# Sharing the re-layout of two inputs among three engines in a batched X times Y-transposed kernel

## The chip, the cores and the metric

The kernel runs on one core of one Trainium2 chip. The metric is the time of one execution on the device in microseconds (us); of several executions the median is given. Engines are called as in the profile: PE is TensorE, DVE is VectorE, ACT is ScalarE, POOL is GpSimd, SP is SyncE, which here only issues transfers (DMA).

## The reference

```python
batch, n_heads, seq_t, seq_s, channels = 8, 12, 512, 512, 64
def reference(x, y):
    return np.einsum('bhtc,bhsc->bhts', x, y).astype(np.float32)
```

For each of 96 heads a 512 x 64 matrix is multiplied with the transpose of another. The inputs are 12.6 MB each, the output 100.7 MB, all float32.

## The kernel before

**Groups and slots.** The 96 heads go in 12 groups of 8. The x and the y of a group are loaded by two transfers of 1 MB into one slot of 16 KB per partition (`load`, L63), x in the first half and y in the second. A head lies on 16 partitions, so a group fills 128. There are five slots (`SLOTS`, L37). Results are collected in slots of the same pool: a result is 2 MB, one slot, one store.

**From a slot to the matmul.** `compress(g)` (L69) casts x to bf16 on ACT (L73, `xk`) and y to bf16 on DVE (L74, `yk`), both 128 partitions x 2048. After that the slot may be used again. Each group has two half groups of four heads (partitions 0 to 63 and 64 to 127); half group i is half i % 2 of group i // 2. `mix(i)` (L77) copies, on GpSimd, the channels of a half group into a layout in which two 32-channel halves lie on different partitions. For x these are four copies of 32 partitions x 1024 (L87) into `xb`, one of two tiles that were zeroed at the start and are used again by every second half group. For y these are two copies of 64 partitions x 1024 (L94) into `yb`. In `xb` and `yb` two bf16 values share one 32-bit word, and `transposes(i)` (L100) then transposes 32 x 32 blocks of words on DVE (L103 for x, L108 for y) into `xT` and `yT`. It also starts the mixing of half group i + 2.

**Results.** A half group gives two results, o = 2i and 2i + 1 (`result(o)`, L115). A result takes eight matmuls, in pairs into four PSUM tiles. ACT copies three of these tiles into a slot (L130) and DVE one (L128). An even result is followed by `transposes(i + 2)` on DVE. Then SP stores the slot (L133).

**Order.** All engines run their instructions in the order in which the program writes them. The five first loads come first (L136). Then for each group (L141): `compress`, at group 0 the mixing of half groups 0 and 1, at groups 2 and 4 the transposes of half groups 0 and 1, a further load at groups 0 to 4, 6 and 8, and results 0, 1 and 2 at groups 5, 7 and 9. The stores of these three results are issued only after the last load (L154). From there the results go one after the other, each with its store (L156). All loads and stores are on SP's queue.

Of the kernel before, what the change touches and what calls it, by code (L numbers as in the profile page):

```python
# [1 line left out]

# [4 lines left out]


@with_exitstack
def kernel(  # L10
    ctx: ExitStack,
    tc: tile.TileContext,
    x: bass.AP,
    y: bass.AP,
    out: bass.AP,
):

    nc = tc.nc
    B, H, T, C = x.shape
    _, _, S, _ = y.shape
    P = 128
    G = 8  # L30
    Q = P // G
    R = T // Q
    NG = B * H // G
    K = 8
    E = R // K
    D = 32
    SLOTS = 5  # L37
    fp32 = mybir.dt.float32
    bf16 = mybir.dt.bfloat16
    u32 = mybir.dt.uint32  # L40
    COPY = mybir.ActivationFunctionType.Copy
    assert C == 2 * D and S == T and R == D and Q * 2 == D

    xv = x.rearrange("b h t c -> (b h t c)").rearrange("(g p n) -> g p n", p=P, n=R * C)
    yv = y.rearrange("b h t c -> (b h t c)").rearrange("(g p n) -> g p n", p=P, n=R * C)
    ov = out.rearrange("b h t s -> (b h t s)").rearrange(
        "(o u h q n) -> o h q u n", u=2, h=2, q=Q * E, n=K * S
    )

    const = ctx.enter_context(tc.tile_pool(name="const", bufs=1))  # L50
    kept = ctx.enter_context(tc.tile_pool(name="kept", bufs=NG))
    slots = ctx.enter_context(tc.tile_pool(name="slots", bufs=SLOTS))
    ybpool = ctx.enter_context(tc.tile_pool(name="ybpool", bufs=2))
    tpool = ctx.enter_context(tc.tile_pool(name="tpool", bufs=3))
    pmpool = ctx.enter_context(tc.tile_pool(name="pmpsum", bufs=4, space=bass.MemoryType.PSUM))

    loaded, inputs, mixed, made = {}, {}, {}, {}
    zeroed = [const.tile([P, K * E * D], u32, name=f"xb{half}") for half in range(2)]

    def slot():  # L60
        return slots.tile([P, K * S], fp32, name="slot")

    def load(g):  # L63
        both = slot()
        nc.sync.dma_start(both[:, :R * C], xv[g])  # L65
        nc.sync.dma_start(both[:, R * C:], yv[g])  # L66
        loaded[g] = both

    def compress(g):  # L69
        both = loaded.pop(g)  # L70
        xk = kept.tile([P, R, C], bf16)
        yk = kept.tile([P, R, C], bf16)
        nc.scalar.activation(xk.rearrange("p r c -> p (r c)"), both[:, :R * C], COPY)  # L73
        nc.vector.tensor_copy(yk.rearrange("p r c -> p (r c)"), both[:, R * C:])  # L74
        inputs[g] = (xk, yk)

    def mix(i):  # L77

        g, half = divmod(i, 2)
        xk, yk = inputs[g]  # L80
        xb = zeroed[half]
        xv2 = xb.bitcast(bf16).rearrange("p (k e c u) -> p k e c u", k=K, e=E, u=2)
        base = half * 64
        for ch in range(2):
            for u in range(2):
                lo = base + u * D
                nc.gpsimd.tensor_copy(  # L87
                    xv2[(2 * ch + u) * D:(2 * ch + u + 1) * D, :, :, :, u],
                    xk[lo:lo + D, :, ch * D:(ch + 1) * D].rearrange("p (e k) c -> p k e c", k=K),
                )  # L90
        yb = ybpool.tile([P, R // 2 * D], u32)
        yv2 = yb.bitcast(bf16).rearrange("p (j c w) -> p j w c", j=R // 2, w=2)
        for ch in range(2):
            nc.gpsimd.tensor_copy(  # L94
                yv2[ch * 64:(ch + 1) * 64],
                yk[base:base + 64, :, ch * D:(ch + 1) * D].rearrange("p (j w) c -> p j w c", w=2),
            )
        mixed[i] = (xb, yb)

    def transposes(i):  # L100
        xb, yb = mixed.pop(i)
        xT = tpool.tile([P, K * D * E], u32)
        nc.vector.transpose(  # L103
            xT.rearrange("p (k r e) -> p k e r", k=K, e=E),
            xb.rearrange("p (k e c) -> p k e c", k=K, e=E),
        )
        yT = tpool.tile([P, D * R // 2], u32)
        nc.vector.transpose(  # L108
            yT.rearrange("p (r j) -> p j r", r=D), yb.rearrange("p (j c) -> p j c", c=D)
        )  # L110
        made[i] = (xT.bitcast(bf16).rearrange("p (k h m) -> p k h m", k=K, h=2), yT.bitcast(bf16))
        if i + 2 < 2 * NG:
            mix(i + 2)

    def result(o):  # L115

        i, h = divmod(o, 2)
        xT, yT = made[i]
        otf = slot()
        ot = otf.rearrange("p (r s) -> p r s", s=S)  # L120
        for k in range(0, K, 2):
            pm = pmpool.tile([P, 2, S], fp32)
            for two in range(2):
                nc.tensor.matmul(  # L124
                    pm[:, two, :], xT[:, k + two, h, :], yT[:, h * S:(h + 1) * S], start=True, stop=True
                )
            if k == 4:
                nc.vector.tensor_copy(ot[:, k:k + 2, :], pm)  # L128
            else:
                nc.scalar.activation(ot[:, k:k + 2, :], pm, COPY)  # L130
        if h == 0 and 2 <= i + 2 < 2 * NG:
            transposes(i + 2)
        return lambda: nc.sync.dma_start(ov[i, h], otf)  # L133

    with tc.manual_schedule():
        for g in range(SLOTS):  # L136
            load(g)
        nc.vector.memset(zeroed[0], 0.0)  # L138
        nc.gpsimd.memset(zeroed[1], 0.0)  # L139
        stores = []  # L140
        for g in range(NG):  # L141
            compress(g)
            if g == 0:
                mix(0)
                mix(1)
            if g in (2, 4):
                transposes(g // 2 - 1)
            if g < 5:
                load(g + SLOTS)
            elif g in (5, 7, 9):  # L150
                stores.append(result(len(stores)))
            elif g in (6, 8):
                load(g // 2 + 7)
        for store in stores:  # L154
            store()
        for o in range(len(stores), 4 * NG):  # L156
            result(o)()


# [1 line left out]
_INS = ['x', 'y']  # L161
_OUTS = [((8, 12, 512, 512), 'float32')]


# [23 lines left out]
```

## Time and profile before

| what | value |
|---|---|
| median of 5 runs | 303.24 us (302.9 to 303.28) |
| the profiled execution | 303.24 us, its span 301.0 us |
| bytes read and written | 25.17 MB and 100.66 MB, 418 GB/s over the span |
| L73 ACT cast of x, x12 | 1.91 us each |
| L74 DVE cast of y, x12 | 1.20 to 2.07 us each |
| L87 POOL copy of x, x96 | 135.5 us, 1.41 us mean |
| L94 POOL copy of y, x48 | 66.0 us, 1.38 us mean |
| L103 and L108 DVE transposes, x24 each | 2.07 and 1.06 us each |
| L130 ACT eviction, x144 | 1.02 us each |
| L128 DVE eviction, x48 | 1.22 us each |
| store, from issue to landing | 21.7 us at the median |

The span runs from the first to the last instruction of the profiled execution; the rest of its time lies around it. Busy time is that of the instructions of an engine; a group of instructions is one line of the program with one shape. The share of the transfer engines is the mean over the core's 16.

### The profile page before, as it was taken

The numbers are of one execution on the slowest core, as the hardware profiler recorded it, in microseconds if no ns is written. First come the engines' busy times: TensorE is split into PE (matmuls) and PEld (weight loads), VectorE is DVE, ScalarE is ACT, GpSimd is POOL, SyncE is SP. The second block draws the span as 40 slices with busy tenths as digits, with TensorE's granted clock in tenths as the row PEclk, the third lists the DMA queues.
The fourth block names the chain that finished last, engine by engine and source line by source line (L and its number), as shares of the span: only waits on it lengthen the run. The fifth ranks groups of instructions, "written<-read, shape, count | busy, mean of one in ns | idle before, by whom it ended". The sixth has DMA issues, their size and how long they took to land.

```text
span 301.0 us, 1574 instructions
## 1 busy us (share of the span) xinstructions
PE 138.2 (46%) x384; PEld 47.0 (16%) x384; DVE 147.1 (49%) x109; ACT 160.8 (53%) x157; POOL 202.6 (67%) x149
## 2 busy tenths in 40 slices
PE   0004124467465556454647554646564658652000
PEld 0001001112121212121212121212121212210000
DVE  1465962857375546653574357535653475313000
ACT  4252567697473747465655465655556564647000
POOL 1999999998997887779776977797779720000000
PEclk9999999569758697786897689778779765779555
DMA  7999999999999999999999999999999999999993
GB/s 290 427 422 422 422 422 422 420 442 425 437 427 425 440 418 438 433 427 438 422 431 439 422 431 431 427 444 418 433 434 425 435 431 420 434 427 425 427 438 144
DMA packets 10377, 125.93 MB, mean 418 GB/s; under 512 B 1152, under 2 KB 1152, under 8 KB 1152
## 3 DMA queue, kind: packets, MB, share of 16 engines
q1 hardware_dynamic: 10368, 125.83, 98.5%
q8 instruction: 3, 0.05, 0.1%
q14 instruction: 6, 0.05, 0.0%
HBM read 25.17 MB, written 100.66 MB: 418 GB/s over the span
## 4 chain that ended last, share of the span: by engine, by line
DMA 82%; ACT 7%; issue 3%; DVE 0%; ACTq 0%; SPq 0%
DMA out_dram<-slot 65%; DMA slot<-in_y_dram 17%; ACT slot L130 7%; DVE yk L74 0%; ACTq L183 0%; SPq L65 0%; SPq L66 0%; ACTq L130 0%
## 5 line engine op out<-in xcount | busy, mean ns | idle before, releaser
L124 PE MATMUL pm<-yT,xT 128*128 128x512 bf16 x384 | 138.2, 513 | 136.3 <-ACT slot L130 112.6
L130 ACT ACTIVATE slot<-pm 128x1024 f32<-128x1024 f32 x144 | 137.0, 1024 | 95.1 <-DMA out_dram<-slot 86.2
L87 POOL COPY xb<-xk 32x1024 bf16<-32x1024 bf16 x96 | 135.5, 1411 | 37.0 <-DVE xT L103 27.4
L128 DVE COPY slot<-pm 128x1024 f32<-128x1024 f32 x48 | 58.8, 1224 | 101.5 <-DMA out_dram<-slot 98.8
L124 PEld LDWEIGHTS <-xT 128*128 128x128 bf16 x384 | 47.0, 122 | 227.1 <-issue 191.8
L94 POOL COPY yb<-yk 64x1024 bf16<-64x1024 bf16 x48 | 66.0, 1375 | 2.9
L103 DVE STREAM_TRANSPOSE xT<-xb 128x1024 uint32<-128x1024 uint32 x24 | 49.6, 2066 | 0.0
L73 ACT ACTIVATE xk<-slot 128x2048 bf16<-128x2048 f32 x12 | 23.0, 1913 | 22.2 <-DMA slot<-in_x_dram 22.2
L74 DVE CAST yk<-slot 128x2048 bf16<-128x2048 f32 x12 | 19.7, 1639 | 27.6 <-DMA slot<-in_y_dram 27.6
L108 DVE STREAM_TRANSPOSE yT<-yb 128x512 uint32<-128x512 uint32 x24 | 25.4, 1058 | 0.0
L73 ACT ACT_TABLE_LOAD x1 | 1.3, 1283 | 0.7 <-PEq L172 0.7
L138 DVE MEMSET xb<- 128x1024 uint32 x1 | 0.9, 912 | 1.0 <-PEq L172 1.0
L139 POOL MEMSET xb<- 128x1024 uint32 x1 | 1.0, 952 | 0.3 <-POOLq L172 0.3
L172 POOL MEMSET const-float32-0.0<- 128x1 f32 x1 | 0.1, 98 | 0.2 <-issue 0.2
L172 POOL MEMSET const-float32-1.0<- 128x1 f32 x1 | 0.1, 98 | 0.0
L172 POOL MEMSET const-bfloat16-1.0<- 128x1 bf16 x1 | 0.1, 98 | 0.0
L172 POOL MEMSET const-uint8-127<- 128x1 uint8 x1 | 0.1, 98 | 0.0
## 6 DMA issues: line engine op xcount, KB each, us to landing
out_dram<-slot SPq DMA_DIRECT2D x48, 2048.0 KB, 21.7
slot<-in_x_dram SPq DMA_DIRECT2D x12, 1024.0 KB, 18.2
slot<-in_y_dram SPq DMA_DIRECT2D x12, 1024.0 KB, 19.2
```

Of the source, the lines that this page charges most:

```text
L73: nc.scalar.activation(xk.rearrange("p r c -> p (r c)"), both[:, :R * C], COPY)
L74: nc.vector.tensor_copy(yk.rearrange("p r c -> p (r c)"), both[:, R * C:])
L87: nc.gpsimd.tensor_copy(xv2[(2 * ch + u) * D:(2 * ch + u + 1) * D, :, :, :, u], xk[lo:lo + D, :, ch * D:(ch + 1) * D].rearrange("p (e k) c ...
L94: nc.gpsimd.tensor_copy(yv2[ch * 64:(ch + 1) * 64], yk[base:base + 64, :, ch * D:(ch + 1) * D].rearrange("p (j w) c -> p j w c", w=2),)
L103: nc.vector.transpose(xT.rearrange("p (k r e) -> p k e r", k=K, e=E), xb.rearrange("p (k e c) -> p k e c", k=K, e=E),)
L108: nc.vector.transpose(yT.rearrange("p (r j) -> p j r", r=D), yb.rearrange("p (j c) -> p j c", c=D))
L124: nc.tensor.matmul(pm[:, two, :], xT[:, k + two, h, :], yT[:, h * S:(h + 1) * S], start=True, stop=True)
L128: nc.vector.tensor_copy(ot[:, k:k + 2, :], pm)
L130: nc.scalar.activation(ot[:, k:k + 2, :], pm, COPY)
L138: nc.vector.memset(zeroed[0], 0.0)
L139: nc.gpsimd.memset(zeroed[1], 0.0)
L172: nc = _bacc.Bacc("TRN2", target_bir_lowering=False, num_devices=1)
```

## The change

- `compress(g)` no longer casts y into `yk`. It casts y from the slot straight into `yb`, the layout that `mix` made before, for both half groups, in four pieces of 64 partitions x 1024: two on DVE, one on GpSimd, one on ACT (`in_front`). `yb` is kept for all groups, in the place of `yk`, and `ybpool` goes.
- `mix` copies x alone, and is told which engines to use and which channel halves to do.
- Half groups 0 to 5 are mixed by GpSimd alone, in the loop over the groups: half group g // 2, channel half g % 2, so two copies per group, behind GpSimd's cast of y.
- Half groups 6 to 23 are mixed after an odd result, half group i + 4 after the second result of half group i: two copies on DVE, one on GpSimd, one on ACT (`behind`).
- `transposes(i)` starts no mixing any more. The transposes of half groups 2 and up stay after even results.

```diff
-    ybpool = ctx.enter_context(tc.tile_pool(name="ybpool", bufs=2))
...
+    in_front = [nc.vector, nc.gpsimd, nc.vector, nc.scalar]
+    behind = [nc.vector, nc.gpsimd, nc.scalar, nc.vector]
+    FIRST = NG // 2
+
+    def copy(engine, dst, src):
+        if engine is nc.scalar:
+            nc.scalar.activation(dst, src, COPY)
+        else:
+            engine.tensor_copy(dst, src)
...
     def compress(g):
         both = loaded.pop(g)
         xk = kept.tile([P, R, C], bf16)
-        yk = kept.tile([P, R, C], bf16)
         nc.scalar.activation(xk.rearrange("p r c -> p (r c)"), both[:, :R * C], COPY)
-        nc.vector.tensor_copy(yk.rearrange("p r c -> p (r c)"), both[:, R * C:])
-        inputs[g] = (xk, yk)
+        inputs[g] = xk
+        ys = both[:, R * C:].rearrange("p (r c) -> p r c", c=C)
+        for half in range(2):
+            yb = kept.tile([P, R // 2 * D], u32, name=f"yb{half}")
+            yv2 = yb.bitcast(bf16).rearrange("p (j c w) -> p j w c", j=R // 2, w=2)
+            for ch in range(2):
+                copy(
+                    in_front[2 * half + ch],
+                    yv2[ch * 64:(ch + 1) * 64],
+                    ys[half * 64:(half + 1) * 64, :, ch * D:(ch + 1) * D].rearrange(
+                        "p (j w) c -> p j w c", w=2
+                    ),
+                )
+            mixed[2 * g + half] = yb
 
-    def mix(i):
+    def mix(i, engines, halves=(0, 1)):
...
-        for ch in range(2):
+        for ch in halves:
             for u in range(2):
-                lo = base + u * D
-                nc.gpsimd.tensor_copy(
+                lo = half * 64 + u * D
+                copy(
+                    engines[2 * ch + u],
                     xv2[(2 * ch + u) * D:(2 * ch + u + 1) * D, :, :, :, u],
                     xk[lo:lo + D, :, ch * D:(ch + 1) * D].rearrange("p (e k) c -> p k e c", k=K),
                 )
-        yb = ybpool.tile([P, R // 2 * D], u32)
-        yv2 = yb.bitcast(bf16).rearrange("p (j c w) -> p j w c", j=R // 2, w=2)
-        for ch in range(2):
-            nc.gpsimd.tensor_copy(
-                yv2[ch * 64:(ch + 1) * 64],
-                yk[base:base + 64, :, ch * D:(ch + 1) * D].rearrange("p (j w) c -> p j w c", w=2),
-            )
...
     def transposes(i):
-        xb, yb = mixed.pop(i)
+        xb, yb = zeroed[i % 2], mixed.pop(i)
...
-        if i + 2 < 2 * NG:
-            mix(i + 2)
...
-        if h == 0 and 2 <= i + 2 < 2 * NG:
+        if h == 0 and i + 2 < 2 * NG:
             transposes(i + 2)
+        elif h == 1 and FIRST <= i + 4 < 2 * NG:
+            mix(i + 4, behind)
...
             compress(g)
-            if g == 0:
-                mix(0)
-                mix(1)
+            mix(g // 2, [nc.gpsimd] * 4, (g % 2,))
```

## The prediction

> **What bounds the kernel now.** I read the page's first two parts, then the stage table, then the queue of transfers, then the load stage in order of time. The page first: busy time by engine, the row of transfer engines in 40 slices, and the share of the one queue that moves data.
>
> ```profile
> PE 138.2 (46%) x384; PEld 47.0 (16%) x384; DVE 147.1 (49%) x109; ACT 160.8 (53%) x157; POOL 202.6 (67%) x149
> ...
> DMA  7999999999999999999999999999999999999993
> ...
> q1 hardware_dynamic: 10368, 125.83, 98.5%
> ```
>
> No compute engine is over 67% busy, while the transfer engines are over 90% busy in 38 of 40 slices. The stage table (busy us and count per engine, then clock, DMA share, GB/s):
>
> ```profile
> 0.00:4.00 4.00, 0.00 (x0) 0.00 (x0) 0.91 (x1) 1.28 (x1) 1.15 (x5) 1.00 0.52 168
> 4.00:24.00 20.00, 1.27 (x4) 0.55 (x5) 9.50 (x6) 7.64 (x4) 15.96 (x11) 1.00 1.02 426
> 24.00:60.00 36.00, 12.94 (x30) 4.20 (x29) 23.11 (x17) 21.59 (x16) 34.92 (x21) 0.91 1.01 422
> ...
> 80.00:244.00 164.00, 92.45 (x267) 31.62 (x266) 87.48 (x66) 94.47 (x100) 132.22 (x101) 0.78 1.01 431
> 244.00:292.00 48.00, 19.63 (x52) 6.43 (x50) 12.87 (x11) 20.27 (x22) 0.00 (x0) 0.64 1.00 427
> 292.00:301.00 9.00, 0.00 (x0) 0.00 (x0) 0.00 (x0) 0.00 (x0) 0.00 (x0) 0.50 0.46 197
> ```
>
> Between 4 and 292 us the transfer engines are full. In the stage 244 to 292 GpSimd does nothing at all and the rate is 427 GB/s, against 431 before it: relieving GpSimd does not speed the transfers. All bytes stay the same, so only a hole in the stream of transfers can change the time by much. I therefore look for the place where the stream is nearest to a hole. That is the end of the load stage, in SP's queue, where each line is start, length, issuing line:
>
> ```profile
> 32.89 0.33 SPq L66 DMA_DIRECT2D slot<-in_y_dram  x1
> 40.35 0.33 SPq L65 DMA_DIRECT2D slot<-in_x_dram  x1
> 40.72 0.43 SPq L66 DMA_DIRECT2D slot<-in_y_dram  x1
> 49.18 0.33 SPq L65 DMA_DIRECT2D slot<-in_x_dram  x1
> 49.55 0.43 SPq L66 DMA_DIRECT2D slot<-in_y_dram  x1
> 50.03 7.63 SPq L133 DMA_DIRECT2D out_dram<-slot  x3
> ```
>
> Loads 10 and 11 are issued here (40.35 and 49.18), each when a slot is free: load 10 takes the slot of group 6, load 11 that of group 8 (slots go in the order in which the program gives them back: 0 to 4 feed loads 5 to 9, 5 feeds result 0, 6 load 10, 7 result 1, 8 load 11). The first three stores stand behind load 11 on SP, though results 0 and 1 are done by then.
>
> **How late may load 11 be?** The engines that wait for the landings show them:
>
> ```profile
> 5.57 1.91 ACT L73 ACTIVATE xk<-slot 128x2048 bf16<-128x2048 f32 x1 [3.56 <-DMA slot<-in_x_dram]
> ...
> 47.80 1.32 DVE L74 CAST yk<-slot 128x2048 bf16<-128x2048 f32 x1 [2.32 <-DMA slot<-in_y_dram]
> ...
> 60.23 1.91 ACT L73 ACTIVATE xk<-slot 128x2048 bf16<-128x2048 f32 x1 [1.33 <-DMA slot<-in_x_dram]
> ```
>
> The x of group 0 was issued at 0.73 into an empty queue and landed at 5.56: 4.83 us. The x of group 11 landed at 60.23, so without a hole it has to be issued by 60.23 - 4.83 = 55.40. It went at 49.18, 6.2 us early. Landings are 2.48 us apart (8.04, 10.54, 13.02), so x of group 10 lands at 55.2 and must go by 50.4; it went at 40.35, 10 us early. Stores have more: they land 21.7 us after issue at the median, and one alone would take about 4.83 + 2.48 = 7.3 (an estimate from the load, for twice the bytes): 14 us of reserve.
>
> **The change part by part.** *Removed:* 12 DVE casts of y (L74, 19.7 us), 48 GpSimd copies of y (L94, 66.0 us), and 54 of 96 GpSimd copies of x. *Added at the load of each group:* y casts of 64 partitions x 1024, float32 to bf16: two on DVE, one on GpSimd, one on ACT. *Moved:* GpSimd's x copies of half groups 0 to 5 now go two per group, behind its y cast; the other 18 half groups' copies are two on DVE, one each on ACT and GpSimd, behind the evictions of an odd result. SP's queue gets nothing new; no transfer is added. What is new is a wait: a slot comes free only when all of ACT's x copy, both DVE casts, GpSimd's cast and ACT's cast have read it. Queued behind it are SP's next load and, behind that, the stores, and result 0, 1 and 2, whose evictions block ACT and DVE in order.
>
> *GpSimd.* No row has a float32 source on it. The row of the same shape and output in this stage (4 to 60 us) is L94 at 1.59 us mean (1.32 at the median of the whole run); x copies are 1.69 there. Ends: 0.95, the GpSimd memset of 1024 words (L139), and 3.18, twice L94 for twice the source bytes. I take 1.59, the nearest row: same count, same output pattern. A group then costs 1.59 + 2 x 1.69 = 4.97, against a landing every 4.96: GpSimd keeps pace, with no reserve. Its cast of group g ends 1.6 us after y landed.
>
> *DVE.* Ends per y cast: 0.62, half of the whole cast when undisturbed (1.23), and 2.07, the longest whole cast. I take 1.23, which is also the 1.22 of L128 for 1024 elements. *ACT:* 1.02 by L130 (1024 elements); ends 0.95 (half of L73) and 1.91 (all of it).
>
> Now the pinch, in order. y5 lands 32.89. DVE casts it to 35.4, ACT evicts result 0 from 35.4 to 38.3 (2.86), DVE its part to 36.6. The transposes of half group 2 wait for GpSimd: 32.9 + 4.97 = 37.9, then 2.07 + 1.06 to 41.0. y6 landed at 37.9, but its casts stand behind them on DVE: 43.5. Load 10 goes at 43.5, limit 50.4. DVE casts y7 to 46.0, which frees the slot of result 1. ACT has meanwhile done x6 (40.2), y6 (41.2), x7 (43.1) and y7 (44.1); it evicts result 1 from 46.0 to 48.9, then x8 to 50.8, y8 to 51.8. GpSimd has y8 done at 49.5 and DVE at 50.3. Load 11 goes at **51.8**: 2.6 us later than now, 3.6 us before its limit. The cover is the loads already queued; it shrinks from 6.2 to 3.6, and nothing reaches the end. Ends: ACT at 1.91 puts load 11 at about 52.7, no cost. DVE at 2.07, reckoned the same way from group 4 (its own queue then never catches up), puts it at 57.7: 2.3 us of hole. GpSimd at 3.18: 8.05 + 9 x 3.18 + 16 x 1.69 = 63.7, 8.3 us of hole. At 0.62 and 0.95 nothing is gained, as the loads do not move faster.
>
> *After the loads.* A half group has two stores; from 77.59 to 275.84 the chain lands 40 stores, 4.96 us each, so 9.91 us. DVE: 2 x 1.22 + 2.08 + 1.07 + two x copies (no DVE row; same ends, 0.62 to 2.07) = 6.8 to 9.7. ACT: 6 x 1.02 + 1.02 (to 1.91) = 7.1 to 8.0. GpSimd 1.32, from 8. PE unchanged. All stay under 9.91 at either end, with 14 us of reserve above that: cost nothing, hidden by the stores. Were that cover gone, DVE's two copies of 1.2 would cost 2.5 us a half group.
>
> [...] Between 4 and 60 us the same DVE cast takes 1.20 to 2.07 and L94 1.30 to 2.19, so the two disturb each other. [...]
>
> **The sum.** The profiled execution took 303.24 us, span 301.0 and 2.24 around it, equal to the median of the five runs. 303.24 + 0 = **303.2**.
>
> **Rivals.** *Slower: GpSimd's cast holds the slots.* Load 11 misses its limit from 8.05 + 9y + 27.0 = 55.4 on, y = 2.26 us, and each 0.1 us over that costs 0.9. At 2.6 the hole is 3.1 (306.3), at 3.18 it is 8.3 (311.5). For it: four bytes a source element where every row has two, and some copies already take 2.2 to 2.5. Against: 2.26 is 1.4 times the mean of a row with the same element count and output. 21%. *Slower: DVE's two casts.* From about 1.7 us each; 305.5 at 2.07. For it, the casts of 1.9 to 2.07 at full size; against, half the elements. 7%. *Faster: the tail.* From 292 on 1.77 MB (197 GB/s x 9) would take 4.2 us at 427, so it could end at 296.2 plus some 2.4 of latency (4.83 - 2.48), near 298.6, not 301.0; a few transfer engines straggle. If a different order of issue evened them, 300.8 to 302.6. Running the loads from 24 to 60 at 426 instead of 422 would give only 36 x 4/426 = 0.3. Against: nothing in the change touches how stores are spread. 10%. *That it does not share:* should casts into one tile run one after another, GpSimd starts 1.23 later once, load 11 goes at about 53, and the time is 303.2: inside the forecast.
>
> **Numbers.** No change 62%, slower 28%, faster 10%; 0.2%, 0.6 us, is about what a measurement of this kernel can tell from no change. Range 302.5 to 306.0: it takes in DVE's end and the first part of GpSimd's, and leaves out about a tenth on each side. For no change alone: 302.6 to 303.8.
>
> **What would show it.** Right: the row of transfer engines stays at 9 from the second slice to the last but one, load 11's x is issued between 50 and 55, GpSimd's busy time falls to about 2.1 + 12 x 1.59 + 24 x 1.69 + 18 x 1.32 = 85 us, and results still wait for store landings. Wrong: SP waiting on GpSimd or DVE at load 11 past 55.4 with a slice of transfers below 9 near 58 us, GpSimd's y cast over 2.26, DVE's over 1.7, or a last store that lands earlier with the same bytes.

## The result and the profile after

The changed kernel takes **302.54 us** (median of 24 runs, 302.23 to 302.71) against 303.2 us before (44 runs); the ratio is 0.9979, 95% interval 0.9974 to 0.9985. The forecast was no change at 303.2. The kernel is faster by 0.66 us, 0.2%. That is 0.04 us inside the stated range (302.5 to 306.0) and 0.06 us outside the band that I had given for no change (302.6 to 303.8).

The page of the changed kernel, the same three rows as before:

```profile
PE 134.8 (45%) x384; PEld 45.7 (15%) x384; DVE 189.7 (63%) x157; ACT 201.1 (67%) x187; POOL 81.9 (27%) x59
...
DMA  7999999999999999999999999999999999999993
...
q1 hardware_dynamic: 10368, 125.83, 98.6%
```

GpSimd went from 202.6 to 81.9 us busy, DVE and ACT took up 43 and 40 us, and the row of the transfer engines did not move by a digit. The stage table says the same (columns as before):

```profile
4.00:24.00 20.00, 0.50 (x2) 0.33 (x3) 10.81 (x9) 12.59 (x8) 15.31 (x10) 1.00 1.01 425
24.00:60.00 36.00, 12.52 (x30) 4.09 (x29) 31.98 (x23) 28.84 (x23) 33.51 (x23) 0.69 1.01 421
...
80.00:244.00 164.00, 92.74 (x274) 31.58 (x273) 116.40 (x103) 119.58 (x119) 22.48 (x17) 0.79 1.01 431
244.00:292.00 48.00, 18.86 (x52) 6.07 (x50) 12.77 (x11) 20.06 (x22) 0.00 (x0) 0.64 1.00 427
```

425, 421, 431 and 427 GB/s stand where 426, 422, 431 and 427 stood. The last two loads on SP's queue, with the first stores behind them:

```profile
43.57 0.33 SPq L74 DMA_DIRECT2D slot<-in_x_dram  x1
43.95 0.43 SPq L75 DMA_DIRECT2D slot<-in_y_dram  x1
53.32 0.33 SPq L74 DMA_DIRECT2D slot<-in_x_dram  x1
53.70 0.42 SPq L75 DMA_DIRECT2D slot<-in_y_dram  x1
54.17 26.36 SPq L145 DMA_DIRECT2D out_dram<-slot  x7
```

Load 10 goes at 43.57 (40.35 before) and load 11 at 53.32 (49.18). Loads are later and yet nothing is lost.

**Where the 0.66 us came from.** For the most part not from the span. The span is 300.78 us on average with the change (25 runs) and 300.76 to 300.82 without it (69 runs in three later batches). What lies around the span fell from 2.22 to 1.78 us: 0.44 of the 0.66. The other 0.2 belongs to no part of the change that the record shows: the spans of the 44 runs behind 303.2 are not on record, and in the three later batches the same kernel has medians of 302.90 to 303.04, so one batch can differ from another by as much. Each execution is known only by its time and its span, but the packets of the profiled executions give a hint. Beside q1, which moves the data, the pages of both kernels have these two rows, which they put down as instructions:

```profile
q8 instruction: 3, 0.05, 0.1%
q14 instruction: 6, 0.05, 0.0%
```

So blocks of code travel on queues of their own, 16 KB a block on q8 and 8 KB on q14, and the kernel before has one more such block behind its last instruction. Read from the two traces, times from the first instruction:

```
before: q14 8 KB at 81.5, 91.9, 96.7, 159.3, 221.1, 256.0 and 302.0 us (0.49 us long); q8 16 KB at 94.8, 174.3, 254.1
after:  q14 8 KB at 78.6, 79.2, 82.1, 144.4, 216.0, 221.1 us;                          q8 16 KB at 94.3, 174.6, 254.4
```

The span of the kernel before ends at 301.0. So at 302.0, 1.0 us later (the expectations below say 1.3), one more block of code was moved, 8 KB in 0.49 us. The experiments test whether this is the cause.

### The profile page after: what moved, and what is told of

The parts are those of the page before. It is cut to its first block, busy times and chain, and to the rows that moved or that the text cites. A ratio compares the mean times of both kernels' runs of the same rounds, so it can differ in the third digit from the quotient of the medians.

```text
span 300.8 us, 1496 instructions
## 1 busy us (share of the span) xinstructions
PE 134.8 (45%) x384; PEld 45.7 (15%) x384; DVE 189.7 (63%) x157; ACT 201.1 (67%) x187; POOL 81.9 (27%) x59
## 4 chain that ended last, share of the span: by engine, by line
DMA 66%; DVE 13%; ACT 10%; issue 2%; PE 1%; ACTq 0%; SPq 0%; DVEq 0%
DMA out_dram<-slot 57%; DMA slot<-in_y_dram 9%; ACT slot L140 8%; DVE yb L67 5%; DVE xT L115 3%; DVE slot L138 2%; ACT xk L82 1%; DVE yT L120 1%; PE pm L134 1%; ACT yb L65 1%; DVE xb L67 0%; ACTq L193 0%; SPq L74 0%; DVEq L138 0%; ACTq L140 0%
## 5 line engine op out<-in xcount | busy, mean ns | idle before, releaser
L134 PE MATMUL pm<-yT,xT 128*128 128x512 bf16 x384 | 134.8, 500 | 139.5 <-ACT slot L140 103.0
L67 POOL COPY xb<-xk 32x1024 bf16<-32x1024 bf16 x42 | 62.2, 1481 | 145.5 <-DVE xT L115 144.4
L134 PEld LDWEIGHTS <-xT 128*128 128x128 bf16 x384 | 45.7, 119 | 228.1 <-issue 190.3
L67 DVE CAST yb<-slot 64x1024 bf16<-64x1024 f32 x24 | 35.2, 1465 | 13.5 <-DMA slot<-in_y_dram 13.2
L67 DVE COPY xb<-xk 32x1024 bf16<-32x1024 bf16 x36 | 26.4, 732 | 0.5
L65 ACT ACTIVATE xb<-xk 32x1024 bf16<-32x1024 bf16 x18 | 24.0, 1336 | 0.4
L67 POOL CAST yb<-slot 64x1024 bf16<-64x1024 f32 x12 | 18.8, 1568 | 8.0 <-DMA slot<-in_y_dram 7.3
L65 ACT ACTIVATE yb<-slot 64x1024 bf16<-64x1024 f32 x12 | 15.9, 1325 | 3.6 <-DMA slot<-in_y_dram 3.4
```

The source lines that it names most:

```text
L65: nc.scalar.activation(dst, src, COPY)
L67: engine.tensor_copy(dst, src)
L134: nc.tensor.matmul(pm[:, two, :], xT[:, k + two, h, :], yT[:, h * S:(h + 1) * S], start=True, stop=True)
```

## The experiments

**The two halves of the change.** The first leaves all x copies on GpSimd, the second leaves y as it was and shares only x.

```diff
-    behind = [nc.vector, nc.gpsimd, nc.scalar, nc.vector]
+    behind = [nc.gpsimd] * 4
```

> The y half of the change alone: y is cast into its layout when it is loaded, as in the changed kernel, but all x copies stay on GpSimd (113 busy instructions there, against 149 before and 59 after). Theory S (the stream of transfers sets the time, and the 0.66 us that the change gained comes from small shifts in the stream): load 11 is issued at 53 us as in the changed kernel and the time is 302.5. Theory G (about two thirds of the gain lies outside the span and goes with the number of instructions on GpSimd): gain 0.66 x 36/90 = 0.26, so 302.9. Theory X (the gain comes from sharing the x copies): 303.2.

```diff
...
-                nc.gpsimd.tensor_copy(
+                copy(
+                    nc.gpsimd if i < 6 else behind[2 * ch + u],
```

> The x half of the change alone: y goes as before (DVE cast, then GpSimd copies), the x copies of half groups 6 to 23 are shared 2:1:1 (95 busy instructions on GpSimd). Load 11 is issued at 49.2 us as before. Theory S: if the later load 11 is what shifted the stream, 303.2. Theory G: 0.66 x 54/90 = 0.40, so 302.8. Theory X: 302.5.

Measured: 302.41 (ratio to before 0.9984, 0.9975 to 0.9992; span 300.69, 1.79 around it) and 302.62 (0.9986, 0.9977 to 0.9995; span 300.76, 1.79 around it). Either half alone takes the 0.44 around the span. A share by the number of GpSimd instructions would have left 2.0 or so in each. Load 11 goes at 53.35 in the first and at 50.16 in the second: theory S fails in the second run and theory X in the first, so neither the late load 11 nor the shared x copies is needed. Neither trace has a code block behind its span.

**Whose block is it?** 24 tiny instructions are added to the kernel before, on one engine at a time, where it waits for the first input. This does no useful work; it only makes that engine's code longer.

```diff
         nc.gpsimd.memset(zeroed[1], 0.0)
+        pad = const.tile([P, 1], fp32, name="pad")
+        for _ in range(24):
+            nc.gpsimd.memset(pad, 0.0)
```

> The kernel before with 24 more tiny GpSimd memsets (128 x 1) at the start, while GpSimd waits for the first input. Its trace has one 8 KB code transfer 1.3 us after the end of the span (0.49 us) that neither the changed kernel nor the two halves show, and 2.2 us around the span against 1.8. Theory F: that late code transfer is waited for and makes the 0.44 us; which engine's code it is depends on where that engine's instructions end against a block. If it is GpSimd's, 24 more instructions move the block's edge into the run: 1.8 around the span, 302.5 to 302.8 in all. If not: 2.2 and 302.9 to 303.2. Theory C (0.44 us go with GpSimd's number of instructions): 2.2 or slightly more here, and 303.0 to 303.3.

The same with `nc.vector.memset`:

> The kernel before with 24 more tiny DVE memsets at the start. Theory F: if the late code transfer is DVE's, 1.8 around the span and 302.5 to 302.8; if not, 2.2 and 302.9 to 303.2. Theory C: 2.2.

The same with 24 ACT copies of 128 x 1:

> The kernel before with 24 more tiny ACT copies at the start (and one DVE memset). Theory F: if the late code transfer is ACT's, 1.8 around the span and 302.5 to 302.8; if not, 2.2 and 302.9 to 303.2. Theory C: 2.2.

| run | time us | ratio to before (95%) | span, mean | around it | code block after the span |
|---|---|---|---|---|---|
| GpSimd padded | 302.60 | 0.9985 (0.9976 to 0.9994) | 300.83 | 1.79 | none |
| DVE padded | 302.97 | 0.9997 (0.9988 to 1.0006) | 300.78 | 2.21 | at 301.9, 0.51 us |
| ACT padded | 302.91 | 0.9999 (0.9990 to 1.0008) | 300.79 | 2.21 | at 301.9, 0.31 us |

The old kernel with 24 useless GpSimd instructions more gains the same 0.43 us around the span. With GpSimd padded there are still seven 8 KB blocks: the one at 81.5 us now stands at 51.1, and in place of the one at 302.0 a second one stands near 220 us, inside the run, at no cost that shows (span 300.83, in the same batch 300.82 before). With DVE padded it is the blocks at 96.7 and 256.0 that move (to 70.6 and 231.2), with ACT padded those at 91.9 and 221.1 (to 68.8 and 196.4), and the late one stays. The late block is GpSimd's. What is lost does not go with the block's own length: with ACT padded it took 0.31 us and with DVE padded 0.51, and 2.21 us lay around the span in both.

**The other way round.** The changed kernel, with GpSimd filled up to the 196 rows that it has in the old kernel's trace (84 in the changed one), behind its last copy:

```diff
             result(o)()
+        pad = const.tile([P, 1], fp32, name="pad")
+        for _ in range(112):
+            nc.gpsimd.memset(pad, 0.0)
```

> The changed kernel with 112 tiny GpSimd memsets behind its last copy, so that GpSimd has as many instructions (196 rows in the trace) as in the kernel before, and in the rest the changed kernel. If the gain is only where GpSimd's last block of code ends, the late code transfer is back about 1.3 us after the span, 2.2 us lie around the span, and the time is 302.95 to 303.2. Rival (the gain comes from GpSimd's relief or from the new order): 302.5, with 1.8 around the span.

Measured: **303.1 us** (1.0005, 0.9996 to 1.0014), span 300.94, 2.22 around it, and an 8 KB code block at 302.0. The 0.44 us are gone while all of the sharing is still there.

**The limit for load 11.** This was the point at which the prediction could have fallen. First, GpSimd gets two of the four y casts, so that it can't keep pace (load 10 is held back too):

```diff
-    in_front = [nc.vector, nc.gpsimd, nc.vector, nc.scalar]
+    in_front = [nc.vector, nc.gpsimd, nc.vector, nc.gpsimd]
```

> Test of the limit for load 11 (55.4 us). The changed kernel, but GpSimd casts two of the four y pieces of a group and ACT none. GpSimd measured 1.57 us a cast and 1.60 us an x copy in the load stage, so it reads the slot of load 11 at 8.1 + 18 x 1.57 + 16 x 1.60 = 62.0 us, 6.6 us after the limit. If the limit holds: a hole in the transfers near 58 us and 302.5 + 6.6 = 309.1 us (308 to 310). Rival (the stream has more in hand than the limit says, because loads and stores already queued cover it): 302.5 to 303.5.

Measured: 311.0 us (1.0259, 1.0243 to 1.0275), 8.5 more than the changed kernel and above the 308 to 310 expected. Loads 10 and 11 on SP (load 10 too is 1 us past its limit of 50.4):

```profile
51.43 0.33 SPq L74 DMA_DIRECT2D slot<-in_x_dram  x1
51.80 0.43 SPq L75 DMA_DIRECT2D slot<-in_y_dram  x1
62.77 0.33 SPq L74 DMA_DIRECT2D slot<-in_x_dram  x1
```

Its stages (busy PE, PEld, DVE, ACT, POOL, then clock, DMA share, GB/s):

```profile
48.00:52.00 4.00, 0.00 (x0) 0.00 (x0) 3.96 (x5) 1.77 (x1) 3.88 (x3) 1.00 1.00 418
52.00:56.00 4.00, 0.00 (x0) 0.00 (x0) 2.80 (x2) 0.00 (x0) 3.88 (x4) 1.00 0.86 320
56.00:60.00 4.00, 2.92 (x7) 0.99 (x7) 3.92 (x4) 4.00 (x4) 3.88 (x3) 1.00 0.49 207
60.00:64.00 4.00, 0.65 (x2) 0.15 (x1) 3.32 (x2) 2.45 (x2) 3.88 (x3) 1.00 0.06 16
64.00:68.00 4.00, 0.00 (x0) 0.00 (x0) 0.00 (x0) 0.00 (x0) 3.83 (x4) 0.50 0.98 342
```

GpSimd is full in every line (3.8 of 4 us) while the transfer engines fall to 6%: this is what the slower rival would have looked like. The sum of 62.0 for load 11 came within 0.8 us; 8.5 us were lost where 6.6 was expected.

Then load 11 alone is held back, by ACT copying the x half of the slot of group 8 once or twice more:

```diff
+    again = const.tile([P, R * C], bf16, name="again")
...
         inputs[g] = xk
+        for _ in range(1 if g == 8 else 0):
+            nc.scalar.activation(again, both[:, :R * C], COPY)
```

> The limit for load 11 from below. The changed kernel with one more ACT copy of the x half of the slot (1.91 us) in group 8, which holds the slot that load 11 takes. Load 11 was issued at 53.3; it goes at 55.2, at the limit of 55.4: 302.5 to 302.7. Rival (every delay of load 11 costs): 304.4.

> The limit for load 11 from above. As the run before, but two such copies in group 8: load 11 goes at 57.1, 1.7 us after the limit: 304.2 (303.9 to 304.8). Rival (the stream has more in hand than the limit says): 302.5.

Once: load 11 goes at 55.19, and the time is 302.84 (0.9995, 0.9987 to 1.0004; 302.5 to 302.7 was expected), span 301.09. Twice (the second block has the columns of the last table, for 54 to 60 us):

```profile
57.09 0.33 SPq L76 DMA_DIRECT2D slot<-in_x_dram  x1
```

```profile
54.00:56.00 2.00, 0.00 (x0) 0.00 (x0) 1.53 (x1) 1.98 (x2) 2.00 (x2) 0.78 1.01 422
56.00:58.00 2.00, 0.00 (x0) 0.00 (x0) 0.00 (x0) 1.98 (x2) 1.94 (x2) 0.50 0.42 172
58.00:60.00 2.00, 0.00 (x0) 0.00 (x0) 0.00 (x0) 1.98 (x2) 1.41 (x2) 0.50 0.85 287
```

The time is 305.22 (1.0069, 1.0057 to 1.0082), 2.7 above the changed kernel and again more than expected; from 56 to 58 us, where the changed kernel moves 430 GB/s, it is 172. So 53.3 costs nothing that shows, 55.2 about 0.3, 57.1 costs 2.7 and 62.8 costs 8.5. From 57.1 to 62.8 a microsecond late is a microsecond lost; that line meets zero at 54.4. At 55.2 it would give 0.8, and 0.3 was measured. The packets show more: at 200 us the stream of the run with one extra copy is 0.48 MB behind the changed kernel's, 1.1 us at 428 GB/s, and that with two is 1.34 MB behind, 3.1 us, while the last packet of data ends only 0.4 and 2.7 us later, so the tail, in which the transfer engines are mostly idle (mean share 0.16 and 0.03 at the end of the changed kernel, below), is shorter by the rest. By the stream both holes begin near 54.0. My limit of 55.4 was 1.0 to 1.4 us too generous, and the reserve of the changed kernel is 0.7 to 1.1 us, not 2.1.

**The floor under both kernels.** All transfers in the same order, without any computation (stores send zeros):

> The transfers alone, in the same order on the same queue: no casts, copies, transposes, matmuls or evictions; the stores send a tile of zeros. It leaves out the whole computation. If the stream alone sets the time of the changed kernel: 302 to 302.6 with a span of 300 to 300.8. If the kernels lose something beside the stream (a slower start or tail by compute): 299 to 301.5. Outside the span: by theory G less than the 1.8 us of the changed kernel, as hardly any instructions are left; otherwise 1.8 to 2.2.

Measured: 299.6 us, span 297.83, 1.78 around it. It has one code block, at 297.6, at the very end of its span, where it adds nothing around the span. Its end and that of the changed kernel (transfers alone first; its columns are busy DVE and POOL, clock, share, GB/s):

```profile
294.00:296.00 2.00, 0.00 (x0) 0.00 (x0) 1.00 0.85 360
296.00:298.00 2.00, 0.00 (x0) 0.00 (x0) 1.00 0.02 4
```

```profile
294.00:296.00 2.00, 0.00 (x0) 0.00 (x0) 0.00 (x0) 0.00 (x0) 0.00 (x0) 0.50 0.92 393
296.00:298.00 2.00, 0.00 (x0) 0.00 (x0) 0.00 (x0) 0.00 (x0) 0.00 (x0) 0.50 0.16 66
298.00:300.80 2.80, 0.00 (x0) 0.00 (x0) 0.00 (x0) 0.00 (x0) 0.00 (x0) 0.50 0.03 12
```

3 us lie between the two. By the packets the changed kernel is 0.6 us behind at 292 us; the rest is a tail in which the 16 transfer engines are mostly idle (mean share 0.16 from 296 us and 0.03 from 298 on). Is it code that travels between the data? Half of PE's instructions are taken away (odd results send the even result's products again), and in another run PE's instructions alone are added to the transfers:

```diff
+    halved = []
...
-                pm = pmpool.tile([P, 2, S], fp32)
-            for two in range(2):
+            if h:
+                pm = halved.pop(0)
+            else:
+                pm = pmpool.tile([P, 2, S], fp32)
+                halved.append(pm)
+            for two in range(0 if h else 2):
```

> Where the 3 us between the transfers alone (299.6) and the changed kernel (302.5) go. The changed kernel with half of PE's instructions: the second result of each half group sends the products of the first once more (it leaves out the matmuls of every odd result; evictions and stores stay). In the traces the queue q8 moves three blocks of 16 KB (0.95 us each) during the run, q14 six of 8 KB (0.31 each), and the transfers alone have none of them; the last transfers straggle 3 us longer. Theory T: these code blocks go through few of the 16 transfer engines, and the one that carries them ends last. Half of PE's code takes away one or two of the three 16 KB blocks: 300.6 to 301.6. Rival (the tail belongs to the evictions or to the slots): 302.4 to 302.7.

```diff
+        w = const.tile([P, 512], bf16, name="w")
+        nc.vector.memset(w, 0.0)
+        pm = pmpool.tile([P, S], fp32)
+        for _ in range(384):
+            nc.tensor.matmul(pm, w[:, :P], w, start=True, stop=True)
```

> The transfers alone with PE's instructions added: 384 matmuls on a tile of zeros into one PSUM tile, never read. It leaves out everything else. PE's code then goes over q8 during the run. If the three blocks of 16 KB all go through the one transfer engine that ends last, each takes 16 KB / (425/16 GB/s) = 0.62 us of it: 299.6 + 1.9 = 301.5, and a longer tail. If the tail belongs to evictions, slots or waits: 299.6.

Half of PE's instructions: 301.23 us, span 299.50; q8 carried one block instead of three. PE added to the transfers: 300.31 us, span 298.55; q8 carried three. So q8 is PE's code. The first run agrees with theory T (1.3 us for two blocks), the second gives 0.7 us for three where 1.9 was expected. Neither theory fits both: 0.62 us a block on one engine is refuted, and what the blocks themselves cost is not shown, since both runs changed PE's work together with its code, and in the second the blocks came early (at 26, 53 and 81 us against 94, 175 and 254). About 2 us of the 3 stay unexplained.

## Why the prediction was right, and what it missed

- **What bounds the kernel: right.** The row of the transfer engines is the same, the rates of the four stages shown agree within 1 GB/s, and the mean span is the same within 0.04 us.
- **GpSimd's float32 cast: right.** 1.59 us was taken from L94; 1.57 was measured. The bound of twice the row does not apply: four bytes an element cost no more here than two, since undisturbed the cast takes 1.30 to 1.33 us and L94 1.32. GpSimd's busy time came to 81.9 for the 85 forecast; of that sum the first term was 1 us too long (GpSimd's instructions other than copies take 1.1 us before, not 2.1).

The added groups, from the page of the changed kernel:

```profile
L67 DVE CAST yb<-slot 64x1024 bf16<-64x1024 f32 x24 | 35.2, 1465 | 13.5 <-DMA slot<-in_y_dram 13.2
...
L67 DVE COPY xb<-xk 32x1024 bf16<-32x1024 bf16 x36 | 26.4, 732 | 0.5
...
L65 ACT ACTIVATE xb<-xk 32x1024 bf16<-32x1024 bf16 x18 | 24.0, 1336 | 0.4
L67 POOL CAST yb<-slot 64x1024 bf16<-64x1024 f32 x12 | 18.8, 1568 | 8.0 <-DMA slot<-in_y_dram 7.3
L65 ACT ACTIVATE yb<-slot 64x1024 bf16<-64x1024 f32 x12 | 15.9, 1325 | 3.6 <-DMA slot<-in_y_dram 3.4
```

- **DVE's and ACT's casts: under-priced.** DVE took 1.47 us on average (0.72 to 1.77), not 1.23; ACT 1.32, not 1.02. The sign of being wrong that was named for DVE, over 1.7 us, came true for more than half of its casts (median 1.73), though not for their mean. The pinch came in the order that was worked out (load 10 at 43.57, forecast 43.5), and these two terms make load 11 1.5 us later than forecast (53.3 for 51.8). In the load stage of the changed kernel:

```profile
36.86 2.85 ACT L140 ACTIVATE slot<-pm 128x1024 f32<-128x1024 f32 x3 [2.57 <-DVE yb L67]
...
41.10 5.89 DVE L67 CAST yb<-slot 64x1024 bf16<-64x1024 f32 x4
...
47.11 2.85 ACT L140 ACTIVATE slot<-pm 128x1024 f32<-128x1024 f32 x3 [0.83 <-DVE yb L67]
48.24 1.32 POOL L67 CAST yb<-slot 64x1024 bf16<-64x1024 f32 x1
...
49.99 1.91 ACT L82 ACTIVATE xk<-slot 128x2048 bf16<-128x2048 f32 x1
51.92 1.32 ACT L65 ACTIVATE yb<-slot 64x1024 bf16<-64x1024 f32 x1
```

Four DVE casts in a row (y6 and y7) free the slot of result 1 at 47.0, forecast 46.0; ACT evicts, then casts x8 and y8, and load 11 follows at 53.3. GpSimd had y8 done by 49.6 and was not what held it.
- **The limit of 55.4: 1.0 to 1.4 us too late.** A first load into an empty queue (4.83 us for x, 7.3 for x and y) is too kind a measure: in the run with two extra copies load 11 had its last packet 8.8 us after its issue, in the run with two GpSimd casts 9.0. Why it takes longer there is not shown. The hole begins near 54.0, and the time rises from about 54.4 on.
- **After the loads: right.** DVE's x copies took 0.73 and ACT's 1.34, inside the bounds, and GpSimd's 1.32, as taken; the stores hide them.
- **The step that failed: "303.24 + 0", with 2.24 us around the span taken as fixed.** The sum priced only the span, and what moved lies around it, 2.22 us before and 1.78 after. The kernel before has 196 rows of GpSimd in its trace, and all four kernels with 196 have the late block and 2.21 to 2.22 us around the span. Those with 16, 84, 96, 146, 151 and 220 rows have no block that begins behind the span, and 1.75 to 1.81 around it. My reading is that with 196 the end of GpSimd's code falls so that one block more is moved at the close; that it is waited for there, and what it holds, is not shown. The faster rival was given a tenth and a wrong place: the tail of the transfers is as long as it was. That 302.54 still lies inside the range is luck: nothing that the prediction gives for its lower bound of 302.5 stands for the 0.44 us.
- **DVE and GpSimd beside each other.** That the two disturb each other holds in the changed kernel's trace too: DVE's cast spreads from 0.72 to 1.77 us and GpSimd's from 1.30 to 1.78. GpSimd's seven casts that begin inside a DVE cast take 1.70 to 1.78, the other five 1.30 to 1.33. For group 0 all start at one landing: DVE's two casts take 0.73 (from 8.11) and then 1.72 us (from 8.87), beside GpSimd's 1.78 (8.21 to 9.99). The second one ends at 10.58, 0.59 us after GpSimd's, and so it goes on: all 22 DVE casts that begin inside a GpSimd cast or copy end 0.58 to 0.69 us after it, while the two that begin outside one take 0.73 each. By these numbers the two take turns; why is not shown. It cost the load stage part of its reserve, not the kernel its time.

## What to carry to other kernels

Here, with the transfer engines over 90% busy in 38 of 40 slices, work shared out among idle engines was worth nothing inside the span (300.78 us with it, 300.76 to 300.82 without). In such a kernel the question for the forecast is which wait can open a hole: work out how late each load may be issued, and keep a microsecond or two for the estimate, which was 1.0 to 1.4 us too late here. A difference of some tenths of a microsecond has to be split into the span and what lies around it before any cause is named: here 24 useless GpSimd instructions took away 0.43 us around the span. An old kernel with a few useless instructions more is the control that tells such a gain from a real one.

## What the hardware showed that was not expected

- Code travels in blocks on its own queues: PE's in 16 KB, 0.95 to 0.97 us each in the changed kernel's run, those of GpSimd, DVE and ACT in 8 KB, 0.31 to 0.34 us. GpSimd's block inside the run cost nothing that shows (span 300.83 against 300.82), what PE's cost is open, and in all four runs in which one came behind the last instruction about 0.43 us more lay around the span.
- The transfers alone need 299.6 us; both kernels are within about 1.2% of that. Of the 3 us between them and the changed kernel, PE's instructions with their code account for 0.7 us in one run, and half of them for 1.3 us in the other; the cause of the rest, most of it a tail, is open.
